# A third z buffer, operand cells built from z, and activation low parts on GpSimd in an fp32-split Strassen block

## Chip, core and metric

One core of one Trainium2 chip (trn2). The metric is the device time of one execution in microseconds, the median of the runs. Everything is fp32 in the reference. TensorE is given fp32r operands here, each split into a high part (rounded by ScalarE's copy to fp32r) and a low part (the rest), so that a product is three matmuls: high x high, high x low, low x high.

## The reference

A block of a streaming encoder, for 512 frames of 2048 channels:

```python
hn = rmsnorm(h, norm_mix_g)
proj = hn @ w_in + b_in            # 2048 x 10248, split in q, k, v, o, i, f, cb, cc, ch, gm, gc
hm = mlstm_chunkwise(q, k, v, i, f) # 4 heads, normed, times sigmoid(o)
y_m = hm @ w_branch_m               # 1024 x 2048
y_c = (cb * causal_dwconv(cc * ch, conv_w)) @ w_branch_c
merged = sigmoid(gm) * y_m + sigmoid(gc) * y_c
h = h + merged @ w_out              # 2048 x 2048
hn = rmsnorm(h, norm_ffn_g)
u = causal_dwconv(hn @ w_up, ffn_conv_w, ffn_conv_b)   # 2048 x 11008
gate, val = split(u)
h = h + (silu(gate) * val) @ w_down                    # 5504 x 2048
return rmsnorm(h, norm_out_g)
```

## The kernel before, in words

**Products.** Channels lie on the partitions, frames along the columns. Each product is done with seven products of half-size blocks instead of eight (a Strassen-like scheme). An *item* is a pair of 128-row output blocks; a *step* is one item and one group q of four 128-row input blocks. In a step `cell_mm` runs twice (r = 0, 1), each time seven products of three matmuls (lines 229, 230, 231: high x high, high x low, low x high), so 42 matmuls of 256 columns. Results gather in two sets of three PSUM banks, used in turn by item, and in one bank shared by both.

**Operands.** A weight step needs one *raw* tile (128 x 1792): three loads on SyncE's queue, two loads on GpSimd's queue that add into it (line 204), two sums on VectorE (169, 174), two high parts on ScalarE (184) and two low parts on VectorE (188). An activation *cell* (a pair of 128-row blocks, `cell_task`) needs a raw tile too: two loads on SyncE's queue, three VectorE sums (276, 281, 286; for w_up also a scaling on ScalarE, 273 and 274), a high part on ScalarE (290) and a low part on VectorE (293), 1792 columns each. There are six raw tiles in all and eight tiles for finished cells, which stay for a whole phase.

**Evacuation and posts.** When an item's last step is on TensorE, `evac_first` (ScalarE, 245) copies the shared bank into `it.z` and `evac_ops` (VectorE, 251 to 254) form the result there. `it.z` is `zs[num % 2]`, one of two buffers of 128 x 1024. Then the item's *posts* run, small closures on VectorE and ScalarE, at the end of which the result is stored to DRAM on ScalarE's queue (`store`, 146). An item's z cannot be written again before the store of the item two back has read it.

**Phases.** w_in (40 items of four steps, with the mLSTM run beside it in small stages on one spare bank), then w_bc (`YC`, 8 items of two steps), w_bm (`HM`, 8 of two), w_out (`MM`, 8 of four), w_up (`HH`, 43 of four), w_down in three chunks of the contraction (8 items of four, three and three steps), and a last part with plain products. First and last pairs of a phase are interleaved step by step. Between phases the results pass through DRAM: `yc_post` stores gated y_c to `mc_d`; `ym_post` (lines 654 to 668) multiplies by the gate, loads `mc_d` into `z2`, adds, negates the second half and stores to `m_d`; the cells of w_out load `m_d`. `out_post` adds the residual, stores `h_d`, squares, and sums the squares in `z2` for the second norm; the cells of w_up load `h_d`.

**Order.** All is emitted by hand in one loop over steps. While TensorE does step s, the low parts of step s + 1, the sums and high parts of step s + 2, evacuations, and cells are emitted. `phase` gives each cell a place (`spread`, relative to the phase's first step, `after`, and a tile to come free); its sums and high part are emitted two steps before that place, its low part one step before. Loads run ahead as far as six raw tiles allow, and a load waits in its queue for its tile. A *credit* counts VectorE's time: 5.04 a step, less what is emitted (`cost`); posts are taken only while the credit lasts, if the item is urgent, or by `flush` when the z buffer is needed.

Of the kernel before, what the change touches and what calls it, by code (L numbers as in the profile page):

```python
# [49 lines left out]
class Item:  # L50


    def __init__(self, load, nq, xs, post, pre=None):
        self.load, self.nq, self.xs, self.post, self.pre = load, nq, xs, post, pre
        self.p1_start, self.urgent = True, False
        self.set = self.num = self.z = self.buf = None


class Task:


    def __init__(self, load, sums, hi, lo, ready=None):
        self.load, self.sums, self.hi, self.lo, self.ready = load, sums, hi, lo, ready
        self.wh = self.wl = None
        self.raw, self.cost, self.plain = None, (0.8, 2.05), False
# [3 lines left out]
def tile_block(ctx: ExitStack, tc: tile.TileContext, xT, w1, w_v0, w_v1, w_v2, w_bm, w_bc, w_out, w_up, w_down,  # L69
# [62 lines left out]
    gm_d, gc_d, mc_d, m_d, h_d, h2_d = (D_([KD, P, T], s) for s in ("gm_d", "gc_d", "mc_d", "m_d", "h_d", "h2_d"))  # L132
# [124 lines left out]
    def cell_task(xs, c, d, scale=None, key=None):  # L257
# [34 lines left out]
        def lo():  # L292
            V.tensor_sub(t.act[:, NW:], t.raw, f(t.act[:, :NW]))  # L293
            t.raw = None
            xs[t.cell] = t.act
            t.act = None

        t.load, t.sums, t.hi, t.lo, t.new_raw = load, [t3, e, t4], hi, lo, new_raw
        t.cost = (1.35, 1.95)
        t.ready = (lambda: all(k in stored for k in key)) if key else None  # L300
        return t
# [352 lines left out]
    def ym_post(p):  # L654
        def post(it):
            j1, j2 = kpair(p)

            def one():
                SP.dma_start(sb_pair(z2), pair_ap(mc_d, j1, j2))
                V.tensor_mul(it.z, it.z, it.buf[:, :2 * T])  # L660

            def two_():
                V.tensor_add(it.z, it.z, z2)
                b = it.z[:, T:]
                A.activation(b, b, AF.Copy, scale=-1.0)
                store(pair_ap(m_d, j1, j2), sb_pair(it.z), ("m", p))
            return [(1.2, one), (1.2, two_)]
        return post
# [6 lines left out]
    acc = z2  # L675

    def out_post(p):
        def post(it):
            j1, j2 = kpair(p)

            def one():
                residual(it)
                store(pair_ap(h_d, j1, j2), sb_pair(it.z), ("h", p))
                A.activation(acc if p == 0 else it.buf[:, :2 * T], it.z, AF.Square)

            def two_():
                if p:
                    V.tensor_add(acc, acc, it.buf[:, :2 * T])
                if p == 7:
                    cols, rows_pe, rows_post = rows_stages(SIDE, rstd, mC)  # L690
                    side.append((lambda: sum_tokens(SIDE, acc, 2, 4, True, True), cols))
                    side.append((rows_pe, rows_post))
            return [(1.3, one), (1.2, two_)]
        return post
# [40 lines left out]
    def add(items, inter):  # L735

        i = 0
        while i < len(items):
# [4 lines left out]
            for it in group:  # L743
                it.num = len(items_all)
                it.set = it.num % 2
                it.z = zs[it.set]
                items_all.append(it)
# [5 lines left out]
    def phase(items, xs, cells, first_pair=True, last_pair=True, chained=False):  # L753

        inter = ({0} if first_pair else set()) | ({len(items) - 2} if last_pair else set())
        e = len(steps)
        add(items, inter)
        for n, t in enumerate(cells):
            t.cell, t.e, t.xs = n, e, xs
            if n == 7 and chained:  # L760
                for it in items_all[-len(items) - 2:-len(items)]:
                    it.urgent = True
            t.after = e + n - 2 if chained and n > 5 else 0
            t.spread = e + ((-4, -2, -1, 0, 2, 3, 5, 6) if items[0].nq > 2 else (-4, -2, 0, 1))[n]
# [27 lines left out]
    def x_task(c):  # L792
# [20 lines left out]
        def hi():  # L813
# [10 lines left out]
          YC, [cell_task(YC, c, yc_d, None, [("yc", k) for k in kpair(c)]) for c in range(4)])  # L824
    phase([Item(tiles_load(w_bm, *kpair(p)), 2, HM, ym_post(p), load_pair(gm_d, *kpair(p))) for p in range(8)],
          HM, [cell_task(HM, c, hm_d, None, [("hm", k) for k in kpair(c)]) for c in range(4)])
    phase([Item(tiles_load(w_out, *kpair(p)), 4, MM, out_post(p), load_pair(xT, *kpair(p))) for p in range(8)],
          MM, [cell_task(MM, c, m_d, None, [("m", c)]) for c in range(8)], chained=True)

    def up_load(j):  # L830
# [3 lines left out]
          HH, [cell_task(HH, c, h_d, g_ffn, [("h", c)]) for c in range(8)], chained=True)  # L834
# [73 lines left out]
    t.cell, t.e, t.first, t.last, t.after, t.spread, t.xs = "x", e_last, e_last, e_last + 15, 0, 0, plain  # L908
# [8 lines left out]
    for n, t in enumerate(all_cells):  # L917
        if n < 8:
            k = t.cell // 2
        else:  # L920
            k = max(k, all_cells[n - 8].last + 3, t.e - 4, t.after, t.spread)
# [50 lines left out]
    def flush(upto):  # L972
# [4 lines left out]
        flush_late()  # L977
# [97 lines left out]
    for i in range(n_start):  # L1075
        start_sums(order[i + 1])
        for fn in lo_ops(order[i]):
            fn()
# [38 lines left out]
    for s in range(4, len(steps)):  # L1117
# [32 lines left out]
        for t in cells_at.get(s + 2, []):  # L1150
# [3 lines left out]
            his.append(t.hi)  # L1154
# [34 lines left out]
        if main and q == it.nq - 1:  # L1189
            flush(it.num - 2)  # L1190
            if it.pre:
                it.pre(it)
            evac_first(it)
# [5 lines left out]
        if s >= 4 + hold:  # L1199
            credit = min(credit, 2.5)  # L1200
            while posts and (credit > posts[0][0] / 2 or posts[0][2] in urgent or not main):
# [87 lines left out]
```

## Time and profile before

| | us |
|---|---|
| median of 3 runs | 2841.49 (2838.44 to 2846.11) |
| profiled execution | 2842.29 |
| its span | 2840.5 |
| TensorE matmuls busy | 2606.6 (92%) |
| VectorE busy | 2213.0 (78%) |
| ScalarE busy | 1294.4 (46%) |
| GpSimd busy | 853.8 (30%) |

The mean granted TensorE clock is 0.963. DMA moved 642.36 MB, 226 GB/s over the span. In the rows below, a group reads: line, engine, operation, output<-inputs, shapes, count, then busy us and mean ns of one, then idle time of the engine before them and what ended it. A wait reads: who waited, for what, us in total, times, longest. A window reads: from:to, length, then busy us of PE, PEld, DVE, ACT and POOL with their counts, granted clock, DMA share and GB/s. PE is TensorE, DVE VectorE, ACT ScalarE, POOL GpSimd, SP SyncE.

### The profile page before, as it was taken

The page shows a single profiled execution, that of the slowest core. Times are in us where ns is not written, and L with a number is a line of the kernel's source. Part 1 is how long each engine was busy: PE and PEld are TensorE (multiplying, and loading weights), DVE is VectorE, ACT ScalarE, POOL GpSimd, SP SyncE. Part 2 cuts the span into 40 slices and gives each one's busy share as a digit, 9 for nine tenths or more (in the row PEclk, how much of TensorE's full clock was granted, in tenths as well). Part 3 has the DMA queues.
Part 4 walks back from the last instruction along what each step waited for, and adds up shares of the span by engine and source line. Part 5 has one row for each costly group of instructions (what it writes and reads, how often), then busy time and mean ns, then how long its engine had stood idle before and what let it go on. Part 6 is the DMA issues. An engine that isn't in the chain of part 4 may idle for free.

```text
span 2840.5 us, 55407 instructions
## 1 busy us (share of the span) xinstructions
PE 2606.6 (92%) x20868; PEld 2578.5 (91%) x20868; DVE 2213.0 (78%) x3360; ACT 1294.4 (46%) x1623; POOL 853.8 (30%) x1003
## 2 busy tenths in 40 slices
PE   7899999999999776689799999999999989979798
PEld 6899999999999776689799999999999979979797
DVE  5777768877777775777879988888888887767676
ACT  6444544455544332344545444444444443434343
POOL 3343323333332221132233333333333223222320
PEclk9999999999999888799999999999999999989899
DMA  7799998989898887798788888989888789889886
GB/s 189 177 236 239 235 245 204 248 214 251 225 240 224 229 238 217 205 259 232 220 211 223 221 225 221 227 216 227 221 223 223 203 227 258 235 236 251 225 244 202
DMA packets 504254, 642.36 MB, mean 226 GB/s; under 512 B 46849, under 2 KB 327425, under 8 KB 503985
## 3 DMA queue, kind: packets, MB, share of 16 engines
q1 hardware_dynamic: 326512, 451.78, 50.4%
q0 software_dynamic: 141536, 125.09, 30.1%
q10 hardware_dynamic: 35936, 61.95, 6.0%
q8 instruction: 163, 2.67, 0.4%
q14 instruction: 107, 0.87, 0.1%
HBM read 576.78 MB, written 61.87 MB: 225 GB/s over the span
## 4 chain that ended last, share of the span: by engine, by line
PE 71%; DMA 11%; DVE 9%; issue 3%; ACT 1%; POOL 0%; SPq 0%; DVEq 0%; POOLq 0%; ACTq 0%
PE bank L229 23%; PE bank L231 23%; PE bank L230 23%; DVE wl L188 3%; DMA h_d<-z 2%; DMA raw<-in_w_down_dram 2%; DVE act L293 2%; DMA z<-mc_d 1%; DMA raw<-in_w_out_dram 1%; DMA raw<-in_w_up_dram 1%; DMA mc_d<-z 1%; DMA raw<-in_w_dram 1%; DMA m_d<-z 1%; PE bank L512 1%; DMA raw<-in_w_bc_dram 1%
## 5 line engine op out<-in xcount | busy, mean ns | idle before, releaser
L229 PE MATMUL bank<-act,wh 128*128 128x256 f32 x6664 | 1928.5, 289 | 133.1 <-ACT z L245 118.2
L231 PE MATMUL bank<-act,wl 128*128 128x256 f32 x6664 | 1916.6, 288 | 52.9 <-DVE wl L188 52.8
L230 PE MATMUL bank<-act,wh 128*128 128x256 f32 x6664 | 1912.9, 287 | 2.3 <-DVE act L293 2.3
L229 PEld LDWEIGHTS bank<-act,wh 128*128 128x128 f32 x6664 | 1307.6, 196 | 142.5 <-ACT z L245 123.0
L184 ACT ACTIVATE wh<-raw 128x896 fp32r<-128x896 f32 x952 | 893.7, 951 | 1111.5 <-PE bank L230 723.7
L231 PEld LDWEIGHTS bank<-act,wl 128*128 128x128 f32 x6664 | 1307.4, 196 | 60.7 <-DVE wl L188 60.5
L230 PEld LDWEIGHTS bank<-act,wh 128*128 128x128 f32 x6664 | 1307.9, 196 | 6.4 <-DVE act L293 3.3
L188 DVE TENSOR_TENSOR wl<-raw,wh 128x896 fp32r<-128x896 f32 x952 | 1034.2, 1087 | 223.4 <-PE bank L231 159.4
L204 POOL DMA_DIRECT2D raw<-in_w_up_dram x344 | 298.9, 951 | 603.2 <-DMA raw<-in_w_up_dram 247.3
L204 POOL DMA_DIRECT2D raw<-in_w_dram x288 | 250.7, 947 | 552.6 <-DMA raw<-in_w_dram 305.3
L169 DVE TENSOR_TENSOR raw<-raw 128x256 f32<-128x256 f32 x476 | 199.6, 419 | 59.6 <-DMA raw<-in_w_down_dram 23.7
L204 POOL DMA_DIRECT2D raw<-in_w_down_dram x160 | 139.4, 986 | 346.4 <-DMA raw<-in_w_down_dram 195.1
L174 DVE TENSOR_TENSOR raw<-raw 128x256 f32<-128x256 f32 x476 | 199.0, 418 | 0.2
L251 DVE TENSOR_TENSOR z<-bank,z 128x512 f32<-128x512 f32 x131 | 90.0, 687 | 101.1 <-ACT z L245 99.5
L290 ACT ACTIVATE act<-xraw 128x1792 fp32r<-128x1792 f32 x52 | 88.3, 1698 | 80.8 <-DVE xraw L286 78.0
L245 ACT ACTIVATE z<-bank 128x256 f32<-128x256 f32 x131 | 48.5, 370 | 145.8 <-DMA h_d<-z 65.2
L293 DVE TENSOR_TENSOR act<-xraw,act 128x1792 fp32r<-128x1792 f32 x52 | 105.0, 2019 | 0.0
L204 POOL DMA_DIRECT2D raw<-in_w_out_dram x64 | 55.7, 971 | 156.4 <-DMA raw<-in_w_out_dram 95.8
L554 DVE TENSOR_TENSOR z<-z,rstd 128x1024 f32<-128x1024 f32 x83 | 101.0, 1218 | 0.0
L252 DVE TENSOR_TENSOR z<-bank,z 128x512 f32<-128x512 f32 x131 | 89.7, 684 | 0.3
L254 DVE TENSOR_TENSOR z<-bank,z 128x512 f32<-128x512 f32 x131 | 89.6, 684 | 0.0
L204 POOL DMA_DIRECT2D raw<-in_w_bm_dram x32 | 27.9, 991 | 112.2 <-DMA raw<-in_w_bm_dram 84.4
(202 smaller groups left out, 1240.6 us busy)
## 6 DMA issues: line engine op xcount, KB each, us to landing
raw<-in_w_up_dram SPq DMA_DIRECT2D x172, 512.0 KB, 5.6
raw<-in_w_dram SPq DMA_DIRECT2D x144, 512.0 KB, 5.9
raw<-in_w_up_dram SPq DMA_DIRECT2D x344, 128.0 KB, 4.2
raw<-in_w_up_dram POOLq DMA_DIRECT2D x344, 128.0 KB, 5.0
raw<-in_w_down_dram SPq DMA_DIRECT2D x80, 512.0 KB, 5.4
raw<-in_w_dram SPq DMA_DIRECT2D x288, 128.0 KB, 4.0
raw<-in_w_dram POOLq DMA_DIRECT2D x288, 128.0 KB, 5.1
raw<-in_w_down_dram SPq DMA_DIRECT2D x160, 128.0 KB, 4.0
```

Of the source, the lines that this page charges most:

```text
L169: V.tensor_add(x[:, 6], x[:, 5], x[:, 0])
L174: V.tensor_add(x[:, 2], x[:, 6], x[:, 1])
L184: A.activation(seven(t.wh[r]), half(r), AF.Copy)
L188: V.tensor_sub(seven(t.wl[r]), half(r), seven(f(t.wh[r])))
L204: G.dma_start(at(i), a21, accum_op=ALU.add)
L229: PE.matmul(ps, h, xh, start=start, stop=False, skip_group_check=True)
L230: PE.matmul(ps, h, xl, start=False, stop=False, skip_group_check=True)
L231: PE.matmul(ps, l, xh, start=False, stop=last, skip_group_check=True)
L251: return [lambda: V.tensor_add(z[:, 0:4:3], b0, two(z[:, 1])), lambda: V.tensor_add(z[:, 1:3], b1, two(z[:, 3])), lambda: V.tensor_add(z[: ...
L252: lambda: V.tensor_add(z[:, 1:3], b1, two(z[:, 3])),
L293: V.tensor_sub(t.act[:, NW:], t.raw, f(t.act[:, :NW]))
L554: V.tensor_mul(sb_pair(it.z), sb_pair(it.z), two(rstd))
```

## The change

From item 40 on (w_bc and later) z is one of three buffers, the third being `z2`; the kernel flushes the posts of the item three back before an evacuation, those of two back only before a load into mA or mB, and the evacuation is emitted ahead of that load. `ym_post` keeps only the product with the gate; `m_d` is gone. The cells of w_out are made by `direct_cell`: they load `mc_d` into the raw tile and add `it.z` to it on VectorE. The last three cells of w_up are scaled by ScalarE straight from z. Such items are urgent, and such a cell's place is at least four steps after its item's last step. Places of the cells of w_bm and w_out move earlier. The sum of squares is kept in `mC`, 512 wide. The low part of every cell made by `cell_task`, but for the first eight of w_in, is subtracted by GpSimd, emitted right behind ScalarE's high part; it counts nothing in the credit.

```diff
--- before.py
+++ after.py
...
         self.load, self.nq, self.xs, self.post, self.pre = load, nq, xs, post, pre
-        self.p1_start, self.urgent = True, False
+        self.p1_start, self.urgent, self.done = True, False, False
         self.set = self.num = self.z = self.buf = None
...
         self.wh = self.wl = None
-        self.raw, self.cost, self.plain = None, (0.8, 2.05), False
+        self.raw, self.cost, self.plain, self.after_end, self.lo_early = None, (0.8, 2.05), False, None, None
...
     so_d, cb_d, yc_d, hm_d = (D_([8, P, T], s) for s in ("so_d", "cb_d", "yc_d", "hm_d"))
-    gm_d, gc_d, mc_d, m_d, h_d, h2_d = (D_([KD, P, T], s) for s in ("gm_d", "gc_d", "mc_d", "m_d", "h_d", "h2_d"))
+    gm_d, gc_d, mc_d, h_d, h2_d = (D_([KD, P, T], s) for s in ("gm_d", "gc_d", "mc_d", "h_d", "h2_d"))
     a_d = D_([NF, P, T], "a_d")
...
         def lo():
-            V.tensor_sub(t.act[:, NW:], t.raw, f(t.act[:, :NW]))
             t.raw = None
...
+        def lo_early():
+            (V if t.by_v else G).tensor_sub(t.act[:, NW:], t.raw, f(t.act[:, :NW]))
+
         t.load, t.sums, t.hi, t.lo, t.new_raw = load, [t3, e, t4], hi, lo, new_raw
-        t.cost = (1.35, 1.95)
+        t.lo_early, t.by_v = lo_early, False
+        t.cost = (1.35, 0)
         t.ready = (lambda: all(k in stored for k in key)) if key else None
+        return t
+
+    def direct_cell(xs, c, it, d=None, scale=None, key=None):
+
+        t = cell_task(xs, c, d, None, key)
+        cell_t3, cell_load = t.sums[0], t.load
+        k1, k2 = kpair(c)
+
+        def load():
+            if d is not None:
+                cell_load()
+            else:
+                t.new_raw()
+
+        def t3():
+            assert it.done
+            a, b = t.raw[:, 5 * SW:], t.raw[:, :2 * SW]
+            if d is not None:
+                V.tensor_add(a, a, it.z[:, :T])
+                V.scalar_tensor_tensor(b, it.z[:, T:], -1.0, b, op0=ALU.mult, op1=ALU.subtract)
+            else:
+                A.activation(a, it.z[:, :T], AF.Copy, scale=scale(k1))
+                A.activation(b, it.z[:, T:], AF.Copy, scale=scale(k2))
+            it.z_read = True
+            cell_t3()
+
+        it.z_read = False
+        t.load, t.sums = load, [t3] + t.sums[1:]
+        t.cost = (2.7, 0) if d is not None else t.cost
+        t.after_end = it
         return t
...
         def post(it):
-            j1, j2 = kpair(p)
-
-            def one():
-                SP.dma_start(sb_pair(z2), pair_ap(mc_d, j1, j2))
+            def fn():
                 V.tensor_mul(it.z, it.z, it.buf[:, :2 * T])
-
-            def two_():
-                V.tensor_add(it.z, it.z, z2)
-                b = it.z[:, T:]
-                A.activation(b, b, AF.Copy, scale=-1.0)
-                store(pair_ap(m_d, j1, j2), sb_pair(it.z), ("m", p))
-            return [(1.2, one), (1.2, two_)]
+                it.done = True
+            return [(1.2, fn)]
         return post
...
-    acc = z2
+    acc = mC
...
                 store(pair_ap(h_d, j1, j2), sb_pair(it.z), ("h", p))
-                A.activation(acc if p == 0 else it.buf[:, :2 * T], it.z, AF.Square)
+                A.activation(it.buf[:, :2 * T], it.z, AF.Square)
+                it.done = True
...
                 if p:
-                    V.tensor_add(acc, acc, it.buf[:, :2 * T])
+                    V.tensor_add(acc, acc, it.buf[:, :T])
+                    V.tensor_add(acc, acc, it.buf[:, T:2 * T])
+                else:
+                    V.tensor_add(acc, it.buf[:, :T], it.buf[:, T:2 * T])
                 if p == 7:
                     cols, rows_pe, rows_post = rows_stages(SIDE, rstd, mC)
-                    side.append((lambda: sum_tokens(SIDE, acc, 2, 4, True, True), cols))
+                    side.append((lambda: sum_tokens(SIDE, acc, 1, 4, True, True), cols))
                     side.append((rows_pe, rows_post))
-            return [(1.3, one), (1.2, two_)]
+            return [(1.3, one), (1.4, two_)]
         return post
...
                 it.set = it.num % 2
-                it.z = zs[it.set]
+                it.z = zs[it.set] if it.num < 40 else (z2, zs[0], zs[1])[(it.num - 40) % 3]
                 items_all.append(it)
...
-    def phase(items, xs, cells, first_pair=True, last_pair=True, chained=False):
-
-        inter = ({0} if first_pair else set()) | ({len(items) - 2} if last_pair else set())
+    def phase(items, xs, cells, spread=(-4, -2, -1, 0, 2, 3, 5, 6), first_pair=True):
+
+        inter = ({0} if first_pair else set()) | {len(items) - 2}
         e = len(steps)
...
         for n, t in enumerate(cells):
-            t.cell, t.e, t.xs = n, e, xs
-            if n == 7 and chained:
-                for it in items_all[-len(items) - 2:-len(items)]:
-                    it.urgent = True
-            t.after = e + n - 2 if chained and n > 5 else 0
-            t.spread = e + ((-4, -2, -1, 0, 2, 3, 5, 6) if items[0].nq > 2 else (-4, -2, 0, 1))[n]
+            t.cell, t.xs, t.spread, t.after = n, xs, e + spread[n], 0
+            if t.after_end:
+                t.after_end.urgent = True
+                t.after = [i for i in range(e) if steps[i][0] is t.after_end][-1] + 4
             use = [s for s in range(e, len(steps)) if steps[s][1] == n // 2]
...
     phase([Item(tiles_load(w_bc, *kpair(p)), 2, YC, yc_post(p), load_pair(gc_d, *kpair(p))) for p in range(8)],
-          YC, [cell_task(YC, c, yc_d, None, [("yc", k) for k in kpair(c)]) for c in range(4)])
-    phase([Item(tiles_load(w_bm, *kpair(p)), 2, HM, ym_post(p), load_pair(gm_d, *kpair(p))) for p in range(8)],
-          HM, [cell_task(HM, c, hm_d, None, [("hm", k) for k in kpair(c)]) for c in range(4)])
-    phase([Item(tiles_load(w_out, *kpair(p)), 4, MM, out_post(p), load_pair(xT, *kpair(p))) for p in range(8)],
-          MM, [cell_task(MM, c, m_d, None, [("m", c)]) for c in range(8)], chained=True)
+          YC, [cell_task(YC, c, yc_d, None, [("yc", k) for k in kpair(c)]) for c in range(4)], (-4, -2, 0, 1))
+    ym_items = [Item(tiles_load(w_bm, *kpair(p)), 2, HM, ym_post(p), load_pair(gm_d, *kpair(p))) for p in range(8)]
+    phase(ym_items, HM, [cell_task(HM, c, hm_d, None, [("hm", k) for k in kpair(c)]) for c in range(4)],
+          (-12, -9, -6, -3))
+    out_items = [Item(tiles_load(w_out, *kpair(p)), 4, MM, out_post(p), load_pair(xT, *kpair(p))) for p in range(8)]
+    phase(out_items, MM, [direct_cell(MM, c, ym_items[c], mc_d, None, [("mc", c)]) for c in range(8)],
+          (-11, -9, -7, -5, 0, 1, 2, 4))
...
     phase([Item(up_load(j), 4, HH, up_post(j)) for j in range(NF)],
-          HH, [cell_task(HH, c, h_d, g_ffn, [("h", c)]) for c in range(8)], chained=True)
+          HH, [direct_cell(HH, c, out_items[c], None, g_ffn) if c > 4 else
+               cell_task(HH, c, h_d, g_ffn, [("h", c)]) for c in range(8)], (-4, -2, -1, 0, 2, 3, 4, 5))
...
     t = last_act()
-    t.cell, t.e, t.first, t.last, t.after, t.spread, t.xs = "x", e_last, e_last, e_last + 15, 0, 0, plain
+    t.cell, t.first, t.last, t.after, t.spread, t.xs = "x", e_last, e_last + 15, 0, e_last - 4, plain
     all_cells.append(t)
...
         else:
-            k = max(k, all_cells[n - 8].last + 3, t.e - 4, t.after, t.spread)
+            k = max(k, all_cells[n - 8].last + 3, t.after, t.spread)
             if tasks[k]:
...
                 posts.popleft()[1]()
-        flush_late()
+            flush_late()
...
         start_sums(order[i + 1])
+        if order[i].lo_early:
+            order[i].by_v = True
+            order[i].lo_early()
         for fn in lo_ops(order[i]):
...
             sms += t.sums
-            his.append(t.hi)
+            his += [t.hi, t.lo_early] if t.lo_early else [t.hi]
         weave(sms, los)
...
         if main and q == it.nq - 1:
-            flush(it.num - 2)
+            if it.num < 42:
+                flush(it.num - 2)
+            flush(it.num - 3)
+            assert it.num < 3 or getattr(items_all[it.num - 3], "z_read", True)
+            evac_first(it)
             if it.pre:
+                flush(it.num - 2)
                 it.pre(it)
-            evac_first(it)
             ended.append(it)
...
             credit = min(credit, 2.5)
-            while posts and (credit > posts[0][0] / 2 or posts[0][2] in urgent or not main):
+            while posts and (credit > posts[0][0] / 2 or any(x[2] in urgent for x in posts) or not main):
                 cost, fn, _ = posts.popleft()
...
```

## Prediction

> **What bounds the kernel now.** I read the page first, for the bound, then the busy time by stretches, then the waits, then the timeline of two stalls. TensorE is the bound by share:
>
> ```profile
> PE 2606.6 (92%) x20868; PEld 2578.5 (91%) x20868; DVE 2213.0 (78%) x3360; ACT 1294.4 (46%) x1623; POOL 853.8 (30%) x1003
> ```
>
> That is a mean over stages. Line 229 runs 14 times a step, so counting it gives each phase's first and last step. The windows view over those bounds (first products with w_bc, w_bm, w_out; the first 14 steps of w_up; the rest of w_up; the three chunks of w_down) gives length, busy time of each engine, granted clock, DMA share and GB/s:
>
> ```profile
> 928.10:1036.50 108.40, 87.19 (x672) 85.97 (x672) 82.86 (x120) 41.14 (x48) 27.54 (x32) 0.92 0.86 240
> 1036.50:1182.10 145.60, 97.50 (x672) 95.49 (x673) 97.29 (x135) 44.48 (x51) 26.19 (x30) 0.79 0.72 204
> 1182.10:1383.40 201.30, 169.94 (x1346) 167.51 (x1344) 149.11 (x211) 86.97 (x96) 55.97 (x65) 0.94 0.90 244
> 1383.40:1483.00 99.60, 83.67 (x607) 81.22 (x608) 79.37 (x119) 46.91 (x54) 31.05 (x36) 0.90 0.83 211
> 1483.00:2283.60 800.60, 797.23 (x6638) 796.42 (x6636) 711.33 (x1037) 390.36 (x478) 267.75 (x309) 1.00 0.88 221
> 2283.60:2473.30 189.70, 169.25 (x1345) 166.81 (x1345) 149.84 (x217) 80.63 (x87) 55.97 (x65) 0.96 0.91 242
> 2473.30:2627.50 154.20, 130.80 (x1008) 129.05 (x1008) 113.71 (x169) 57.26 (x62) 41.70 (x49) 0.92 0.89 241
> 2627.50:2775.30 147.80, 130.14 (x1009) 128.92 (x1010) 108.25 (x159) 53.20 (x61) 38.06 (x44) 0.93 0.87 236
> ```
>
> In the steady stretch (1483.00) 797.23 us hold 6638 matmuls, 0.120 us each; a step of 42 takes 5.04 us and nothing else matters there. At that rate the w_bc, w_bm and w_out phases (64 steps, 322.6 us) took 455.3, an excess of 132.7; the head of w_up (14 steps, 70.6) has 29.0; the w_down chunks (80 steps, 403.2) took 491.7, an excess of 88.5. So 250 us can be reached at all, most densely in w_bm: 145.6 for 80.6.
>
> The waits of PE, asked for 928.1:1383.4, 1383.4:1483.0 and 2283.6:2775.3, say what ends them (us, times, longest):
>
> ```profile
> PE bank L229 <- ACT z L245: 70.6, 12, 10.0
> PE bank L231 <- DVE wl L188: 23.9, 12, 6.3
> ...
> PE bank L229 <- ACT z L245: 3.7, 1, 3.7
> ...
> PE bank L229 <- ACT z L245: 40.0, 9, 7.3
> PE bank L231 <- DVE wl L188: 14.4, 12, 2.7
> ```
>
> L245 is ScalarE's first evacuation of a finished item: 114.3 us in 22 waits. What ScalarE waited for there:
>
> ```profile
> ACT z L245 <- DMA h_d<-z: 65.2, 9, 10.4
> ...
> ACT z L245 <- DMA mc_d<-z: 39.7, 4, 12.7
> ...
> ACT z L245 <- DMA m_d<-z: 18.5, 4, 6.6
> ```
>
> It waits until the store of the item two back has left the z buffer. And each wait leaves the clock low behind it: 0.67 granted over 25 us with two such waits, where matmuls of line 229 come 0.64 us apart, three matmuls in the time of five:
>
> ```profile
> 1175.00:1200.00 25.00, 12.40 (x74) 12.20 (x75) 16.34 (x21) 7.81 (x10) 1.83 (x3) 0.67 0.72 210
> ...
> 1178.40 0.41 PE L229 MATMUL bank<-act,wh 128*128 128x256 f32 x1
> 1179.04 0.41 PE L229 MATMUL bank<-act,wh 128*128 128x256 f32 x1
> ```
>
> PE was busy 12.40 us for 74 matmuls worth 8.9, so a wait costs 1.75 us more than its length.
>
> **The change, part by part.**
>
> *Three z buffers.* L245 now waits for the item three back. A store lands in some 10 us (longest wait 12.7); in the two-step phases one more item is 10 us more, in three- and four-step ones 15 and 20. I take all 114.3 us away, and 22 times 1.75, 38 us, of slow clock: 153 in all, an upper bound, since another wait is next in line. The load into mA or mB now follows the evacuation, so the ACT queue is not held by the posts; the post of two back still precedes that load. The cells' low part costs no credit any more, so posts are issued earlier near phase heads; that is what makes the third buffer useful at the interleaved first pairs.
>
> *Operand cells out of z.* m_d's eight stores and eight loads go; mc_d is loaded into the cell's raw tile instead of z2. Bytes: 8.4 MB less of 104.8 (240, 204 and 244 GB/s times their lengths). Three cells of w_up read z and not h_d. DVE: the 8 additions of 1024 become 16 instructions of 512 (about 0.7 each), even to within 2 us; ScalarE saves 8 negations of 0.63. New wait: a cell needs its item's product first. Behind it on VectorE stand weight sums and low parts, and PE behind those; the cell is placed four steps after its item's last step, so I price it at nothing, and at up to 5 us a phase if VectorE is late.
>
> *What is late next: VectorE in the w_bm phase.* Its rows by line, in 1036.5:1182.1:
>
> ```profile
> L188 DVE TENSOR_TENSOR wl<-raw,wh 128x896 fp32r<-128x896 f32 x34 | 36.9, 1085 | 3.9 <-PE bank L231 3.6 <-issue 0.3
> L293 DVE TENSOR_TENSOR act<-xraw,act 128x1792 fp32r<-128x1792 f32 x5 | 10.1, 2020 | 0.0
> L174 DVE TENSOR_TENSOR raw<-raw 128x256 f32<-128x256 f32 x17 | 7.1, 418 | 0.0
> ...
> L252 DVE TENSOR_TENSOR z<-bank,z 128x512 f32<-128x512 f32 x9 | 6.2, 684 | 0.0
> ...
> L253 DVE TENSOR_TENSOR z<-bank,z 128x256 f32<-128x256 f32 x9 | 3.8, 424 | 0.3
> L660 DVE TENSOR_TENSOR z<-z,mA 128x1024 f32<-128x1024 f32 x3 | 3.7, 1218 | 0.0
> ```
>
> A step takes 2 of L188 and 2 sums: 3.01 us, 48.2 for 16 steps; an evacuation three of 0.684 and one of 0.424, 2.48, 19.8 for 8; a post 1.22, 9.8; six cells of w_out fall here, each 512 + 256 + 256 and two of 512, about 3.0: 18. Together 96 against PE's 80.6. With the phase's head (some 8 us) w_bm comes to 104, not 80.6. The w_bc phase takes over the four sums of the hm cells; VectorE has 48.2 + 19.8 + 9.8 + 6 = 84 there, little over PE.
>
> So for the three phases: 70.6 + 12 x 1.75 = 92 gone, 17 given back to VectorE and raw loads: **-75**, 380 us, in which the remaining 95 MB need 250 GB/s, a little over the 244 they have now. Head of w_up: the one wait with its slow clock and part of the load after store, **-8**. Chunks: 40.0 + 9 x 1.75 = 56; but their 118 MB already ran at 242 and would need 256 GB/s at -30. I take **-30**; the lower end is -10 and the upper -56.
>
> *Low parts on GpSimd.* 44 of the 52 L293 (2.02 us) leave VectorE: 89 us there, of which only those near phase heads are on the path. No two-input subtraction on POOL is in the trace. The nearest rows:
>
> ```profile
> L487 POOL TENSOR_SCALAR_AFFINE_SELECT mA<-mA 128x128 f32<-128x128 f32 x16 | 10.9, 682 | 0.4 <-ACT mA L486 0.4
> ...
> L413 POOL MEMSET mB<- 128x512 f32 x1 | 0.5, 525 | 1.1 <-DVE mC L407 1.1
> ...
> masks.py:199 POOL TENSOR_SCALAR_AFFINE_SELECT identw<-identw 128x128 f32<-128x128 f32 x1 | 0.3, 333 | 0.1
> ```
>
> Bounds for 1792 columns: 1.8 us by the memset, 9.5 by 14 times 682. The select of 333 ns reads and writes like the subtraction and gives 4.7 with 14 starts counted; one start instead brings it near 4. I take 4.0. The Trainium skill (GPSIMD Engine Reference, Performance versus the Vector engine) gives 4497 ns for an addition of 2048 columns; worked out from it, an estimate, 3.9 us. No run here shows it yet.
>
> What stands behind that subtraction on POOL: its wait for ScalarE's high part, then the accumulating DMAs, two per step,
>
> ```profile
> L204 POOL DMA_DIRECT2D raw<-in_w_down_dram x160 | 139.4, 986 | 346.4 <-DMA raw<-in_w_down_dram 195.1 <-DVE raw L174 35.1 <-DVE raw L169 28.4
> ```
>
> so 2.0 us of a step; 4.0 more make 6.0 in a step that has a cell, over 5.04, but POOL is idle 70% and six raw tiles are in flight. VectorE's relief (-2.0 a cell) and the later DMAs (up to +4 a cell) nearly cancel; for 44 cells I take **+15**, with ends -25 and +60.
>
> Sum: -75 - 8 - 30 + 15 = -98, against the profiled execution's 2842.3 us (span 2840.5): 2744. The median of the runs, 2841.5, is 0.8 below; I leave 2744. The squares' sum kept in mC (two additions of 512 for one of 1024), the earlier places of cells, and the stores that wait for a flush move under 2 us each beside other work; if VectorE were full there, 2 us.
>
> **The rivals.**
>
> *VectorE is held while POOL subtracts.* If each subtraction shuts out VectorE's two-input instructions, a cell costs VectorE 4.0 us instead of 2.0, not 0. In the w_bm phase that is 96 + 6 x 4 = 120; at the heads of the others +2 a cell. Two thirds of 44 x 2.0 is 60 given back: -113 + 60 = -53, 2789. One place bears on it, a select inside a subtraction:
>
> ```profile
> 16.52 2.02 DVE L293 TENSOR_TENSOR act<-xraw,act 128x1792 fp32r<-128x1792 f32 x1
> ...
> 18.36 0.33 POOL masks.py:199 TENSOR_SCALAR_AFFINE_SELECT identw<-identw 128x128 f32<-128x128 f32 x1
> ```
>
> Neither is stretched, against the rival; but they share 0.18 us only, and the other order is not shown. The Trainium skill (SBUF — State Buffer, Who interferes with whom) says that a VectorE instruction with two SBUF inputs and a GpSimd one that reads SBUF exclude each other for the whole instruction. By that rule this rival is the forecast; the trace cannot settle it, and the rule is why it has 21%.
>
> *PE's other waits do not grow.* All 153 us come back, and VectorE's waits shrink by 10: 2842 - 163, about 2680. Against it: VectorE's 96 us in w_bm and the DMA rates above. 10%.
>
> *Raw loads take over.* If DMA can give no more than 242 to 244 GB/s, the chunks stay, and if SyncE's queue keeps the earlier phases as they are, the time is 2842. Ten-microsecond windows of steady w_down without a stall speak against it. 4%.
>
> *Slower: POOL's queue becomes the bound.* At a head some 8 cells fall in 10 steps, 50 us; 20 DMAs take 20, so POOL is full at 3.8 us a subtraction. The gain to be eaten is 113 over five heads, 23 each, so it decides from (50 - 20 + 23) / 8 = 6.6 us. At the bound of 9.5, a head is 20 + 76 = 96 us, 46 too long; five are 230, less 113, less what six tiles in flight hide (about 15 a head): near 2885. 8%.
>
> **How the numbers follow.** Forecast 57% (2695 to 2770), VectorE held 21% (2789), no new waits 10% (2680), raw loads 4%, POOL's queue 8%. The range 2695 to 2815 takes the first two and leaves 2 in 10. A difference of 0.3% (8.5 us) is about what a measurement of this kernel can tell from none. Faster 0.88, the same 0.04, slower 0.08.
>
> **What would show it.** Right: PE's waits for ACT z L245 under 15 us; the second window near 104 us; no m_d rows; the subtraction on POOL near 4 us; granted clock over 0.9 in every stretch. Wrong: L188's mean above 1.09 us or gaps on VectorE where POOL subtracts (held); VectorE's sum L169 waiting on raw loads behind a busy POOL (queue); z waits that merely moved to pre-load or post. The prediction fails most easily in POOL's duration and in what of VectorE's relief reaches PE.

## The result, and the profile after

The changed kernel takes 2809.6 us (median of 4 runs, 2807.5 to 2817.4) against 2842.8 for the kernel before: ratio 0.989, interval 0.987 to 0.991. It is 33 us faster; 98 were forecast. The profiled execution has a span of 2815.7 us.

The page's busy times, then the windows of the same phases as in the prediction (their bounds found by counting line 229 again; length, PE, PEld, DVE, ACT, POOL, granted clock, DMA share, GB/s):

```profile
PE 2602.3 (92%) x20860; PEld 2574.3 (91%) x20860; DVE 2274.3 (81%) x3332; ACT 1287.9 (46%) x1615; POOL 1041.7 (37%) x1047
```

```profile
937.60:1048.00 110.40, 90.94 (x673) 89.15 (x674) 100.84 (x127) 43.92 (x51) 51.24 (x40) 0.89 0.91 260
1048.00:1151.70 103.70, 86.66 (x674) 85.64 (x673) 95.63 (x126) 40.17 (x45) 40.35 (x31) 0.92 0.81 225
1151.70:1350.90 199.20, 170.61 (x1347) 169.18 (x1345) 158.54 (x210) 83.44 (x91) 89.69 (x74) 0.94 0.84 227
1350.90:1453.90 103.00, 81.26 (x599) 78.72 (x600) 86.13 (x121) 48.60 (x57) 45.25 (x37) 0.89 0.70 175
1453.90:2264.30 810.40, 798.77 (x6638) 797.88 (x6636) 717.10 (x1029) 388.96 (x475) 287.75 (x316) 1.00 0.87 219
2264.30:2463.90 199.60, 172.12 (x1344) 169.20 (x1344) 159.91 (x209) 79.51 (x86) 90.11 (x73) 0.95 0.85 230
2463.90:2613.40 149.50, 129.37 (x1008) 127.64 (x1008) 118.55 (x163) 57.01 (x62) 68.00 (x55) 0.93 0.91 247
2613.40:2747.30 133.90, 126.13 (x1008) 124.82 (x1009) 110.06 (x156) 52.86 (x61) 46.81 (x45) 0.96 0.94 259
```

Only the w_bm phase fell as forecast (145.6 to 103.7 us), and the last w_down chunk by 14 us. The w_bc, w_out and second w_down windows are within 5 us of what they were; the head of w_up, its long steady part and the first w_down chunk are 3 to 10 us longer. Line 293's 89 us of low parts are gone from VectorE, and yet it is busier in all (2274 us against 2213). PE's waits over these windows have changed owner:

```profile
PE bank L231 <- DVE wl L188: 117.3, 47, 8.6
PE bank L229 <- DVE z L251: 24.4, 5, 6.0
...
PE bank L230 <- POOL act L298: 1.2, 1, 1.2
```

PE hardly waits for GpSimd's low parts themselves (1.2 us). VectorE's own rows, over the whole span, show why it waits for VectorE. Before:

```profile
L188 DVE TENSOR_TENSOR wl<-raw,wh 128x896 fp32r<-128x896 f32 x952 | 1034.2, 1087 | 223.4 <-PE bank L231 159.4
...
L169 DVE TENSOR_TENSOR raw<-raw 128x256 f32<-128x256 f32 x476 | 199.6, 419 | 59.6 <-DMA raw<-in_w_down_dram 23.7
L174 DVE TENSOR_TENSOR raw<-raw 128x256 f32<-128x256 f32 x476 | 199.0, 418 | 0.2
...
L251 DVE TENSOR_TENSOR z<-bank,z 128x512 f32<-128x512 f32 x131 | 90.0, 687 | 101.1 <-ACT z L245 99.5
```

After:

```profile
L188 DVE TENSOR_TENSOR wl<-raw,wh 128x896 fp32r<-128x896 f32 x952 | 1082.7, 1138 | 209.6 <-PE bank L231 144.5
...
L169 DVE TENSOR_TENSOR raw<-raw 128x256 f32<-128x256 f32 x476 | 229.1, 481 | 79.2 <-DMA raw<-in_w_down_dram 36.2
L298 POOL TENSOR_TENSOR act<-xraw,act 128x1792 fp32r<-128x1792 f32 x44 | 190.0, 4318 | 172.0 <-ACT act L290 166.3
L174 DVE TENSOR_TENSOR raw<-raw 128x256 f32<-128x256 f32 x476 | 228.4, 480 | 0.2
...
L251 DVE TENSOR_TENSOR z<-bank,z 128x512 f32<-128x512 f32 x131 | 89.7, 685 | 8.3 <-ACT z L245 6.6
```

The waits for ScalarE's evacuation are over: L251 waits 6.6 us for L245, where it waited 99.5. In their place PE waits for the weights' low parts, L188, whose mean rose from 1087 to 1138 ns; the sums L169 and L174 rose from 419 to 480. L251, which reads one operand from PSUM, is at 685 as before. One stall in the w_bm phase shows two ways in which this happens (POOL's, VectorE's and PE's timelines):

```profile
1088.24 3.97 POOL L298 TENSOR_TENSOR act<-xraw,act 128x1792 fp32r<-128x1792 f32 x1 [6.00 <-ACT act L290]
1092.16 3.54 POOL L204 DMA_DIRECT2D raw<-in_w_bm_dram  x4
...
1088.28 0.42 DVE L253 TENSOR_TENSOR z<-bank,z 128x256 f32<-128x256 f32 x1
1088.62 4.55 DVE L188 TENSOR_TENSOR wl<-raw,wh 128x896 fp32r<-128x896 f32 x1
1093.09 0.68 DVE L254 TENSOR_TENSOR z<-bank,z 128x512 f32<-128x512 f32 x1
...
1099.12 0.42 DVE L169 TENSOR_TENSOR raw<-raw 128x256 f32<-128x256 f32 x1 [3.22 <-issue]
...
1093.22 0.58 PE L231 MATMUL bank<-act,wl 128*128 128x256 f32 x1 [4.43 <-DVE wl L188]
```

First: while POOL subtracts (to 1092.21), L188 does not get on; it takes 4.55 us instead of 1.09, and PE stands 4.43. Second: POOL had waited 6.00 us for ScalarE's high part, so four accumulating DMAs of two weight steps come out only at 1092.16, and the next weights' sum starts at 1099.12 after 3.22 us of idle VectorE. (That row names no cause, only "issue"; that it waited for these DMAs is read from the order.) The experiments were made to price each.

### The profile page after: what moved, and what is told of

It reads as the page before. It is cut to its first block, busy times and chain, and to the rows that moved or that the text cites. A ratio compares the mean times of both kernels' runs of the same rounds, so it can differ in the third digit from the quotient of the medians.

```text
span 2815.7 us, 55373 instructions
## 1 busy us (share of the span) xinstructions
PE 2602.3 (92%) x20860; PEld 2574.3 (91%) x20860; DVE 2274.3 (81%) x3332; ACT 1287.9 (46%) x1615; POOL 1041.7 (37%) x1047
## 4 chain that ended last, share of the span: by engine, by line
PE 42%; issue 7%; DMA 5%; DVE 3%; POOL 2%; SPq 0%; ACT 0%; DVEq 0%; POOLq 0%; ACTq 0%
PE bank L231 14%; PE bank L229 13%; PE bank L230 13%; DMA raw<-in_w_down_dram 2%; DVE wl L188 1%; DMA raw<-in_w_up_dram 1%; POOL raw L204 1%; POOL act L298 1%; DMA mB<-h_d 1%; PE bank L365 0%; PE bank L1039 0%; PE bank L1040 0%; PE bank L1041 0%; DVE xraw L276 0%; DMA raw<-in_w_out_dram 0%
## 5 line engine op out<-in xcount | busy, mean ns | idle before, releaser
L229 PEld LDWEIGHTS bank<-act,wh 128*128 128x128 f32 x6664 | 1304.4, 196 | 36.7 <-DVE z L251 26.0
L188 DVE TENSOR_TENSOR wl<-raw,wh 128x896 fp32r<-128x896 f32 x952 | 1082.7, 1138 | 209.6 <-PE bank L231 144.5
L169 DVE TENSOR_TENSOR raw<-raw 128x256 f32<-128x256 f32 x476 | 229.1, 481 | 79.2 <-DMA raw<-in_w_down_dram 36.2
L298 POOL TENSOR_TENSOR act<-xraw,act 128x1792 fp32r<-128x1792 f32 x44 | 190.0, 4318 | 172.0 <-ACT act L290 166.3
L174 DVE TENSOR_TENSOR raw<-raw 128x256 f32<-128x256 f32 x476 | 228.4, 480 | 0.2
L251 DVE TENSOR_TENSOR z<-bank,z 128x512 f32<-128x512 f32 x131 | 89.7, 685 | 8.3 <-ACT z L245 6.6
L276 DVE TENSOR_TENSOR xraw<-xraw 128x512 f32<-128x512 f32 x52 | 56.0, 1078 | 27.3 <-ACT xraw L835 17.8
L253 DVE TENSOR_TENSOR z<-bank,z 128x256 f32<-128x256 f32 x131 | 55.6, 424 | 4.5
```

Of the source, the lines that this page charges most:

```text
L169: V.tensor_add(x[:, 6], x[:, 5], x[:, 0])
L174: V.tensor_add(x[:, 2], x[:, 6], x[:, 1])
L188: V.tensor_sub(seven(t.wl[r]), half(r), seven(f(t.wh[r])))
L229: PE.matmul(ps, h, xh, start=start, stop=False, skip_group_check=True)
L251: return [lambda: V.tensor_add(z[:, 0:4:3], b0, two(z[:, 1])), lambda: V.tensor_add(z[:, 1:3], b1, two(z[:, 3])), lambda: V.tensor_add(z[: ...
L298: (V if t.by_v else G).tensor_sub(t.act[:, NW:], t.raw, f(t.act[:, :NW]))
```

## The experiments

Ratios are against the kernel before on the same chip, with 95% intervals, three rounds each.

**The z part alone.** Diff against the changed kernel:

```diff
         def lo():
+            V.tensor_sub(t.act[:, NW:], t.raw, f(t.act[:, :NW]))
             t.raw = None
...
-        def lo_early():
-            (V if t.by_v else G).tensor_sub(t.act[:, NW:], t.raw, f(t.act[:, :NW]))
...
-        t.cost = (1.35, 0)
+        t.cost = (1.35, 1.95)
```

(and 1.95 in `direct_cell` likewise)

> The change without its last part: three z buffers, operand cells from z, the new places and flushes, but the low parts of activations back on VectorE, one step after the high part, and priced in the credit. Held theory (a GpSimd subtraction shuts out VectorE's instructions with two SBUF inputs; in the changed kernel's trace such instructions overlapping one are 143 us longer in all, against 89 us of low parts taken off VectorE): the 113 us forecast for this part come back in good part, 2730 to 2770 us. Queue theory (the subtraction delays the accumulating DMAs behind it on GpSimd's queue): the same 2730 to 2770. Third theory, the z part was itself priced too high and the low parts matter little: 2800 to 2815, as the whole change.

2726.8 us, ratio 0.959 (0.957 to 0.961). Its windows for w_bc, w_bm and w_out, the head and the rest of w_up, and the three chunks of w_down:

```profile
926.80:1034.60 107.80, 90.62 (x675) 88.79 (x674) 91.85 (x130) 43.41 (x50) 31.42 (x36) 0.91 0.91 255
1034.60:1130.10 95.50, 85.06 (x674) 83.84 (x673) 90.45 (x132) 40.45 (x46) 24.40 (x28) 0.96 0.92 261
1130.10:1308.30 178.20, 167.66 (x1346) 165.27 (x1344) 147.82 (x217) 82.71 (x91) 53.93 (x63) 0.97 0.92 247
1308.30:1404.20 95.90, 78.15 (x599) 75.88 (x600) 73.89 (x114) 44.13 (x51) 30.84 (x36) 0.91 0.80 200
1404.20:2210.90 806.70, 799.73 (x6638) 798.10 (x6636) 716.73 (x1043) 394.11 (x482) 268.35 (x310) 1.00 0.87 219
2210.90:2396.30 185.40, 169.68 (x1345) 167.24 (x1345) 149.76 (x217) 80.48 (x87) 55.90 (x65) 0.96 0.91 246
2396.30:2528.70 132.40, 125.15 (x1008) 123.93 (x1008) 113.17 (x169) 57.17 (x62) 41.85 (x49) 0.97 0.99 277
2528.70:2661.40 132.70, 125.33 (x1009) 124.32 (x1010) 107.95 (x159) 53.20 (x61) 38.07 (x44) 0.97 0.95 267
```

So the z part brings 119 us of its own (113 forecast), and the low parts on GpSimd take 83 of it back. The third theory, a z part priced too high, has fallen.

**The z part, the low part not charged to the credit.** The same kernel with `t.cost = (1.35, 0)`, and 0 in `direct_cell`.

> As the run with the z part alone, but the low part on VectorE is not charged to the credit, as in the change, so that posts are issued earlier near phase heads. If the earlier posts are what makes the third buffer useful, it is 5 to 20 us faster than the z part alone; if posts were on time anyway, within 5 us of it; if they crowd VectorE before the weights' low parts, up to 10 us slower.

2719.4 us, 0.956 (0.955 to 0.957): 7 us under the z part alone by the medians, in the band expected for earlier posts, though 7 us is little more than the runs can tell apart. It is the fastest complete version here, 90 us below the whole change, and differs from it only in which engine subtracts and when.

**The low parts on GpSimd alone**, on the kernel before:

```diff
-            V.tensor_sub(t.act[:, NW:], t.raw, f(t.act[:, :NW]))
...
+        def lo_early():
+            (V if t.by_v else G).tensor_sub(t.act[:, NW:], t.raw, f(t.act[:, :NW]))
...
-        t.cost = (1.35, 1.95)
+        t.cost = (1.35, 0)
...
-            his.append(t.hi)
+            his += [t.hi, t.lo_early] if t.lo_early else [t.hi]
```

> The kernel before with only the last part of the change: the low parts of the cells subtracted by GpSimd behind ScalarE's high part, not priced in the credit. Held theory: VectorE loses about 143 us and wins 89, mostly at phase heads; the time is 20 to 80 us over the kernel before, 2860 to 2920. Queue theory: slower too, 2860 to 2900. If the low parts matter little: within 10 us of 2842. My forecast of +15 for this part: 2857.

2839.5 us, 0.998 (0.996 to 1.000): no loss, against both theories and against my own 2857; only "the low parts matter little" fits the time. But PE's waits are not those of the kernel before:

```profile
PE bank L231 <- DVE wl L188: 120.0, 50, 8.5
PE bank L229 <- DVE z L251: 30.4, 6, 6.1
PE bank L229 <- ACT z L245: 24.9, 5, 10.4
```

Over the whole span the waits for L245 fell from 118 to 25 us with two buffers, and the L188 waits rose from 53 to 120. Two effects cancel, and this edit has two parts: the subtraction goes to GpSimd, and the low part is no longer charged to the credit. Hence:

**One number: the kernel before with the low part (on VectorE) not charged**, `t.cost = (1.35, 0)` and nothing else.

> The kernel before with one number changed: a cell's low part, still on VectorE, is not charged to the credit. The kernel before with the low parts on GpSimd was only 6 us faster or the same, with PE's waits for the z evacuation fallen from 118 to 25 us. If those waits fell because posts and stores are issued earlier, not because of GpSimd: this kernel has them under 50 us too and runs at 2770 to 2815. If they fell because VectorE was relieved: about 2842 again.

2755.9 us, 0.970 (0.968 to 0.971), a little below the band, with these waits of PE:

```profile
PE bank L231 <- DVE wl L188: 80.7, 42, 9.7
PE bank L229 <- ACT z L245: 26.5, 7, 8.6
```

So 86 us came from posts that are no longer put off: they store z earlier (ScalarE's waits for a z store fall from 135 to 29 us), and two buffers nearly suffice. Beside this kernel, GpSimd's low parts cost 84 us (2839.5 - 2755.9), as they cost 90 beside the z part (2809.6 - 2719.4).

**GpSimd busy, but hardly reading.** In the changed kernel, `lo_early` for the 44 cells becomes

```diff
-            (V if t.by_v else G).tensor_sub(t.act[:, NW:], t.raw, f(t.act[:, :NW]))
+            lo = f(t.act[:, NW:])
+            G.tensor_copy(t.act[:, NW:NW + 1], f(t.act[:, :1]))
+            for _ in range(3):
+                G.memset(lo, 0.0)
```

> The change with each of the 44 subtractions on GpSimd replaced by a copy of one column of the high part (so that GpSimd's queue still waits for ScalarE) and three memsets of the low part, 1792 columns each, about 1.6 us by the memset rows: GpSimd is as busy as with the subtraction, but reads one column only. The cells' low parts are left out (zeros) of the computation. Held theory: VectorE is free of the low parts and is not held; its weights' low part takes 1.09 us again and the time falls to 2690 to 2740. Queue theory: GpSimd's accumulating DMAs are as late as in the change, 2795 to 2815.

2761.3 us, 0.971 (0.969 to 0.972): between the two bands, so both theories hold a part. VectorE is not held (L188 back at 1086 ns), but L169 now waits far more for weights, 162 us in all:

```profile
L188 DVE TENSOR_TENSOR wl<-raw,wh 128x896 fp32r<-128x896 f32 x952 | 1033.1, 1086 | 218.1 <-PE bank L231 153.3
...
L169 DVE TENSOR_TENSOR raw<-raw 128x256 f32<-128x256 f32 x476 | 199.3, 419 | 162.0 <-DMA raw<-in_w_down_dram 72.1
```

Three more kernels take this queue cost apart.

**One memset behind the wait** (`range(1)`):

> The changed kernel with each subtraction on GpSimd replaced by the copy of one column of the high part and one memset (about 2.0 us instead of 5.2 with three memsets); the cells' low parts are left out of the computation. GpSimd's queue still waits for ScalarE's high part, but is occupied shortly. If what the writes-only kernel lost against the z part alone (2761 against 2719) comes from that wait, which stands ahead of the accumulating DMAs: 2745 to 2765. If it comes from GpSimd being occupied: 2700 to 2725. If half and half: 2725 to 2745.

2702.1 us, 0.951 (0.949 to 0.953), in the band for GpSimd's occupation and against the wait as the whole cost.

**Three memsets, no column copied**, so nothing to wait for:

> As the kernel with one column and three memsets, without the copy of the column: GpSimd is occupied 4.8 us a cell, but its queue waits for no high part. The low parts are left out. If the wait for ScalarE is the cost: 2695 to 2725. If the occupation is: 2740 to 2765.

2685.7 us, 0.945 (0.944 to 0.947), under both bands: without the wait even the long occupation costs little.

**One memset, no column:**

> One memset a cell, 1.6 us on GpSimd, no wait for the high part; the low parts are left out. Neither cost is there to speak of, so it shows what taking the low parts off VectorE is worth beside the z part alone (2719): my forecast counted up to 25 us, so 2695 to 2720; if VectorE is not what bounds the phase heads any more, 2712 to 2722.

2665.4 us, 0.938 (0.936 to 0.940), far below what I expected. Its memset took 2.2 us by the mean, not 1.6, so that GpSimd is occupied here as long as with the copied column and one memset (2.0). From the z part with free credit (2719.4) this is 54 us less, twice my upper end of 25. I put the 54 down to VectorE's relief; it also holds that a cell's raw tile comes free once ScalarE has read it, and not only after VectorE's low part, and no run takes the two apart. The wait for the high part, with a copied column, costs 37 (2702.1 - 2665.4). Two memsets more, 3.2 us, cost 20 without the wait and 59 with it: the two multiply. What stands behind them in the queue is the accumulating DMAs of the next weights, and L169's idle time grows with the cost: 55.6, 76.5, 94.3 and 162.0 us for one and three memsets without the wait, and one and three with it.

**The subtraction emitted behind the loads of its step:**

```diff
-            his += [t.hi, t.lo_early] if t.lo_early else [t.hi]
+            his.append(t.hi)
+            if t.lo_early:
+                after_loads.append(t.lo_early)
...
         loads()
+        for fn in after_loads:
+            fn()
```

> The whole change, the subtraction still on GpSimd, but emitted after the loads of its step, so that the accumulating DMAs of that step are ahead of it in GpSimd's queue. Queue theory (order): about 20 to 35 us back, 2775 to 2792. Held theory alone: VectorE is shut out as long as before, 2800 to 2815; its two-input instructions that overlap a subtraction are again some 140 us longer in all.

2800.2 us, 0.986 (0.984 to 0.987): 9 us back, at the edge of the held theory's band and less than half of what the queue theory gave. POOL's wait for ScalarE's high part falls from 166 to 46 us, and L169's idle time from 79 to 38, but the sums are stretched more (502 ns), all instructions that overlap a subtraction are 164 us longer (143 in the change), and SyncE's loads wait 228 us for the subtraction to release a raw tile (165 in the change).:

```profile
POOL act L298 <- ACT act L290: 45.9, 16, 9.3
```

```profile
L188 DVE TENSOR_TENSOR wl<-raw,wh 128x896 fp32r<-128x896 f32 x952 | 1072.4, 1127 | 214.2 <-PE bank L231 148.4 <-issue 60.1 <-ACT wh L184 3.7
L169 DVE TENSOR_TENSOR raw<-raw 128x256 f32<-128x256 f32 x476 | 238.9, 502 | 37.9 <-DMA raw<-in_w_down_dram 17.3 <-DMA z<-in_xT_dram 6.5 <-DMA raw<-in_w_bc_dram 5.9
```

I take it that the longer holding and the later raw tiles ate most of what the order gave back; no run tests that apart.

**As long as the subtraction, and keeping the raw tile as long**: one column of the high part, two memsets, then one column of the raw tile.

> GpSimd waits for the high part (one column copied), writes the low part twice (3.2 us), then copies one column of the raw tile, so that it is occupied about as long as with the subtraction (4.1 to 4.3 us) and keeps the raw tile as long, but reads only two columns. The low parts are left out. Between the kernels with one and with three memsets (2702 and 2761) the occupation alone gives about 2740. If the raw tile's late release is a cost of its own: 2755 to 2790. If the read that shuts out VectorE is the rest of the change's loss: 2730 to 2750, 60 to 80 under the change.

2771.6 us, 0.974 (0.972 to 0.977), in the band for a cost of the late release.

**The same, the last column from the high part instead:**

> As the kernel that reads one column of the raw tile last (2772), but the last column comes from the high part, so that the raw tile is free once ScalarE has read it; GpSimd's wait and occupation are the same, some 4.1 us. The low parts are left out. If the raw tile's late release is a cost of its own, as the interpolation between one and three memsets suggests: 2730 to 2750. If the interpolation is at fault and the occupation is all: 2762 to 2780.

2750.2 us, 0.968 (0.965 to 0.970). The pair differs in one column's source, so 21 us are the raw tile's late release alone (in the band for that): a later load waits for the tile. SyncE's loads wait 105.5 us for POOL's last copy in the first kernel, and never for POOL in the second.

**One input instead of two**: `G.tensor_copy(t.act[:, NW:], f(t.act[:, :NW]))`.

> GpSimd copies the high part into the low part (one input of 1792 columns instead of two); the low parts are left out. If any GpSimd instruction that reads SBUF shuts out VectorE's instructions with two SBUF inputs, those that overlap a copy are stretched to its end again, and with a copy of 2 to 3 us instead of 4.3 the time lies between the kernel with one memset behind the wait and the change: 2730 to 2775. If one input does not shut them out, VectorE's durations stay at 1.09 and 0.42 us and the time is 2700 to 2725.

2715.2 us, 0.955 (0.953 to 0.957), below the band for a hold and in the one for none, but with VectorE stretched: the copy took 1.68 us at the least, and L188 averaged 1104 ns. The instructions that overlap one are 50 us longer in all. One memset behind the same wait (2.0 us, writing only) gave 2702.1; so a reader of about the same length costs 13 us more. This kernel also bears on another doubt: where the low parts are left out, TensorE multiplies by zeros in one matmul of three, here it does not, and the mean granted clock is the same (0.980 beside 0.979).

**The subtraction in four pieces of 448 columns**, behind the loads:

> The kernel with the subtraction behind the loads, in four instructions of 448 columns. If the exclusion is by instruction, VectorE waits for one piece (about 1.1 us) and not for 4.3, and its stretched instructions are more in number but short: 2765 to 2790 against 2800. If GpSimd's pieces win the port each time, VectorE is out for all four: 2795 to 2810.

2825.1 us, 0.993 (0.991 to 0.995): slower than either band. Its VectorE and POOL at one place:

```profile
906.41 6.47 DVE L188 TENSOR_TENSOR wl<-raw,wh 128x896 fp32r<-128x896 f32 x1 [1.00 <-PE bank L231]
...
906.79 5.13 POOL L303 TENSOR_TENSOR act<-xraw,act 128x448 fp32r<-128x448 f32 x4
```

Here one L188 stands through all four pieces, 6.47 us, and in 28 of the 44 cells a VectorE instruction is held until the last piece is done. In the other 16 the two engines take turns: VectorE's instructions run between the pieces, none held longer than 1.1 us, and the four pieces take 5.4 to 7.1 us instead of 4.7 to 5.2. So each band's theory describes a part of the cells. In all 174 us of holding came, against 164 for the same order in one piece.

## Why the prediction was wrong, step by step

*The z part: right in size, in part by luck.* With the low parts on VectorE, w_bc to w_out took 381.5 us (-74; forecast -75), the head of w_up 95.9 (-4; -8), the chunks 450.5 (-41; -30): -119 against -113. (The steady part of w_up took 806.7 for 800.6, which I had put at nothing; so w_up as a whole gained nothing.) z waits under 15 us were forecast for the whole change, and it has 7.2. But the ground that I gave does not hold. I named the credit as what makes the third buffer useful: with the low part still charged the z part gave 119, and freeing the credit 7 more. The one-number kernel shows that the credit alone gives 86 with two buffers. So the two remove largely the same waits, and most of what I read as stores that land late were posts put off for lack of credit. The trace of the kernel before had it: I took "some 10 us" for a store to land, near the longest wait, but its DMA view gives a median of 5.3 us from issue to landing for h_d and 5.5 for mc_d.

*The w_bm phase: right by accident.* 104 was forecast and 103.7 came; with the low parts on VectorE it is 95.5, under my sum of VectorE's work plus a head. The 8 us between are GpSimd's.

*GpSimd's duration: right.* 4.0 us was taken; 3.95 to 4.91, median 4.08, came. The Trainium skill (GPSIMD Engine Reference, Performance versus the Vector engine) gave the estimate 3.9, and the trace agrees.

*The failing step: the term for the low parts, +15 with ends -25 and +60.* It measured +83 beside the paid credit and +90 beside the free one. My own figures a cell, -2.0 and up to +4.0, allowed 88 us for 44 cells; I let them "nearly cancel" and closed the range at +60 without a reason. The change's 2809.6 is reached from the z part with free credit so (medians from several chips, on which the kernel before lies within 4 us):

| step | us | from |
|---|---|---|
| z part, free credit | 2719.4 | |
| VectorE without the low parts, raw tile free earlier | -54.0 | one memset, 2665.4 |
| POOL waits for the high part first | +36.7 | 2702.1 |
| POOL occupied 4.1 us, not 2.0 | +48.1 | high part read last, 2750.2 |
| raw tile kept to the end | +21.4 | raw tile read last, 2771.6 |
| reads whole operands: VectorE shut out, POOL 4.3 us | +38.0 | the change, 2809.6 |

I wrote that relief and later DMAs nearly cancel; the relief was 54, the queue 85 and the raw tile 21, and the 38 of the held VectorE were in the rival only, not in the sum. I had priced the queue as throughput (full from 3.8 us a subtraction, decisive from 6.6). It costs as delay long before it is full. (Why six raw tiles do not cover this delay is not shown; that a cell takes one of them between weight steps is my guess.) Each price holds at its place in the ladder alone: the subtraction behind the loads, which takes most of the wait out of the queue, got 9 us back, not 85.

*The rival that VectorE is held: its mechanism is shown.* Instructions that overlap a subtraction are 143 us longer in all (sum of each one's duration less its line's median, over all VectorE instructions that overlap one of the 44). Its time, 2789, was too low because its sum (-113 + 60) has no term for the queue or the raw tile at all; and its price is less than forecast, 38 us at the end of the ladder for 60. The rule of the Trainium skill behind it (SBUF — State Buffer, Who interferes with whom) agrees in what it names: instructions with two SBUF inputs are stretched (L188 to 1138 ns), L251 with an operand from PSUM is not (685), memsets stretch nothing (L188 at 1086), and a copy with one input does (1104). The select that overlapped a subtraction of VectorE in the kernel before was no evidence: in 0.18 us of overlap nothing could be seen of what 44 subtractions show.

*Raw loads take over: no.* In the z part w_bc to w_out ran at 255, 261 and 247 GB/s and the last two chunks at 277 and 267, so the 242 to 244 that I weighed was no ceiling. (The bytes left for w_bc to w_out are 104.8 - 8.4 = 96.4 MB, not 95.)

*What was forecast of the signs:* L188's mean over 1.09 us and L169 behind a busy POOL were both named as marks of failure, and both came. The signs for "right" came nearly all as well (z waits, w_bm, 4 us a subtraction), for they test the z part and the duration, not what a subtraction delays; the clock stayed above 0.9 in all but two windows (0.89).

## What to carry to other kernels

Before moving work to an engine with idle time, write down what stands behind it in that engine's queue and what it must wait for there: 4 us a cell on a GpSimd that is 30% busy cost 85 us on the ladder above, because each stood behind another engine and ahead of the weights' accumulating DMAs, and 21 more because it kept its input buffer longer. Take GpSimd work that reads SBUF as time taken from VectorE's two-input instructions, and set it against what it relieves: here 89 us of VectorE's work went and 143 us of holding came. What it would be with an empty queue was not tried. And where a hand-written schedule has a price list, test the price before the buffers: one number gave 86 us where a third buffer and a new data path gave 119, and both together gave 126.

## What was not expected of the hardware

VectorE's L188 that began 0.36 us ahead of a subtraction was held all the same (VectorE's and POOL's timelines of the changed kernel):

```profile
917.35 6.01 DVE L188 TENSOR_TENSOR wl<-raw,wh 128x896 fp32r<-128x896 f32 x1
...
917.71 4.69 POOL L298 TENSOR_TENSOR act<-xraw,act 128x1792 fp32r<-128x1792 f32 x1
```

In the changed kernel this is the exception: 25 instructions with both inputs in SBUF began ahead of a subtraction and overlapped it, and 24 of them kept their length while the subtraction took longer (up to 4.91 us, where 3.95 is the shortest); of the 42 that began later, 41 were held. With the subtraction behind the loads 11 of 33 that began ahead were held. So the start in the trace does not always tell which of the two goes first. Cutting GpSimd's work into pieces gives VectorE a turn between them in some cells only (16 of 44), and makes the work longer: four pieces took 4.7 to 7.1 us, one behind the same loads 4.6 by the median. In all, the four-piece kernel was 25 us slower than the same order in one piece. What decides between a turn and none is not settled.
